# Down projection of a decoder layer: 20 of 22 row blocks in seven-product form, the third weight sum made in the block of the product ahead of it

## The chip, the cores and the metric

The kernel runs on one core of a Trainium2 chip. The metric is the device time of one execution in microseconds; the median of three runs is given. The profile is of one more execution.

## The reference

One decoder layer in float32: x is 512 rows of 1024. A token-mixing part (three attention branches, gated and projected) is followed by a gated MLP. The change lies in the last product of the MLP:

```python
x = x + rmsnorm(merged @ w_out[l], norm_mix_post[l])
h = rmsnorm(x, norm_ffn_pre[l])
u = causal_depthwise_conv(h @ w_ffn_up[l], ffn_conv_w[l], ffn_conv_b[l])
u_gate, u_val = jnp.split(u, 2, axis=-1)
y = (jax.nn.gelu(u_gate, approximate=True) * u_val) @ w_ffn_down[l]
x = x + rmsnorm(y, norm_ffn_post[l])
```

The hidden width is 2816, so `w_ffn_down` is 2816 x 1024: 22 row blocks of 128.

## The kernel before

All large products run on TensorE in split precision. A float32 operand is divided into a high part (ScalarE, line 85) and a rest (VectorE, line 86), and each product is three matmuls: high x high, high x rest, rest x high (`mm3`, `down3`). An instruction multiplies 128 x 128 by 128 x 512.

**Down projection.** Output is 512 rows (four blocks t of 128) by two halves h of 512 columns; each (t, h) has a PSUM bank. The first 16 of the 22 row blocks are taken in four groups d of four (NG = 4). Within a group the product is written as a 2 x 2 block product, and the seven-product form of Strassen and Winograd replaces eight block products by seven. A plain group of four row blocks is 4 x 4 x 2 x 3 = 96 matmuls; in the seven-product form it is 7 x 12 = 84. Product n of group d is called (n, d). The order is written out by hand in `seq`: products 1, 5, 6, 2, 7, 3, 4, each for all groups, then the six plain blocks (n = 0).

The sums of activations that the form needs are made on POOL in `sums` (lines 783 to 790), right after the last of a group's four blocks in the up projection: tile G holds the blocks (`gpair`), tile S three sums (`gsum`). The sums of weights are made by DMA: a quarter of a group (128 x 1024 in SBUF, 512 KB) is loaded on SP's queue, and `add_in` (line 859) lets a DMA on POOL's queue add another quarter from HBM into the same tile. Products 1, 5, 6, 4 of a group share one tile, `chain[d]`: it is loaded for 1, and after the split of 1, 5 and 6 the next quarter is added. Products 2, 7, 3 and the plain blocks take the four slots of `raw2` in turn; for product 7 a quarter is loaded into a slot and a second one added to it (lines 873 and 877).

`prepare(i)` issues loads up to three products ahead (`fetch_down`), then splits the weights (tiles whi and wlo, three buffers) and the activations (xh, xl). `upto(i + 2)` runs it two products ahead of TensorE. After the last group of product 1, 5, 6 and 7 ScalarE or VectorE reads the product's banks (lines 942 to 948) into `s_`, `z5` and `u2`, from which the output is put together.

The plain blocks come last. The last four (LATE = 4) are split into tiles of their own and are multiplied row block by row block, in the order t = 2, 3, 0, 1, so that norm, residual and store of one row block (lines 963 to 971) run beside the matmuls of the next.

The order of TensorE's instructions is that of the text. On the other engines the tile framework orders the instructions by a simulation of its own when the program is built, so they can leave the order of the text. The tiles named hT (two buffers) hold the activations of the up projection until its last matmul; after that `raw2` and `xlate` take their place.

Of the kernel before, what the change touches and what calls it, by code (L numbers as in the profile page):

```python
# [11 lines left out]
F32 = mybir.dt.float32  # L12
F32R = mybir.dt.float32r
# [6 lines left out]
P = 128  # L20
# [7 lines left out]
EPS = 1e-6  # L28
BIG = 1e30
VLEN = 640  # L30
LATE = 4
EARLY = 4
NG = 4
NS = 4 * NG
C_QMB, C_KMB, C_VMB, C_QSW, C_KSW, C_QME = 0, 512, 1024, 1536, 2048, 2304
C_GMB, C_GSW, C_GME = 2816, 3840, 4864
# [3 lines left out]
def tile_hybrid_layer(  # L40
# [734 lines left out]
    gpair = [T(fp, [P, 4, SEQ], F32, "G", NG) for _ in range(NG)]  # L775
    gsum = [T(fp, [P, 3, 2, 256], F32, "S", NG) for _ in range(NG)]
    grest = T(fp, [P, NF - NS, SEQ], F32, "gN", 1)

    def quarters(d):

        return [[gpair[d][:, r::2, c * 256 : (c + 1) * 256] for r in range(2)] for c in range(2)]

    def sums(d):

        (a11, a12), (a21, a22) = quarters(d)
        s1, s2, s4 = (gsum[d][:, i] for i in range(3))
# [26 lines left out]
    for f in range(NF):  # L813
        if f == 0:
            for k, banks in enumerate(zip(up_products(0), up_products(1))):
                if k + 4 < KD:
                    turn1(k + 4)
            issue(b_up[EARLY + 1])
        else:
            banks = [list(up_products(2 * f))[-1]]  # L820
        cg = conv(2 * f, banks[0])
        act.activation(cg[:], cg[:], AF.Gelu_apprx_tanh)  # L822
        if f:
            banks.append(list(up_products(2 * f + 1))[-1])
# [23 lines left out]
    u2 = [c_tile() for _ in range(2)]  # L848
    chain = {}
    loaded = {}  # L850
    turn = [0]
# [6 lines left out]
    def add_in(tile_, d, r, c):  # L858
        pool.dma_start(two(tile_), quarter(d, r, c), accum_op=ALU.add)

    seq = [(n, d) for n in (1, 5, 6, 2, 7, 3, 4) for d in range(NG)] + [(0, k) for k in range(NS, NF)]
    first_of = {2: (1, 0), 3: (1, 1), 7: (0, 1)}

    def fetch_down(i):
        n, d = seq[i]
        if n == 1:
            chain[d] = T(wp, [P, 1024], F32, "raw", 4)[:]
            sp.dma_start(two(chain[d]), quarter(d, 0, 0))
        elif n in first_of or n == 0:
            loaded[i] = raw2[:, turn[0] % 4, :]  # L870
            turn[0] += 1
            if n:
                sp.dma_start(two(loaded[i]), quarter(d, *first_of[n]))
            else:
                sp.dma_start(loaded[i], wd[d * P : (d + 1) * P, :])
            if n == 7:
                add_in(loaded[i], d, 1, 1)

    ready = {}
    fetched = [0]  # L880
# [1 line left out]
    def prepare(i):  # L882

        while fetched[0] <= min(i + 3, len(seq) - 1):
            fetch_down(fetched[0])
            fetched[0] += 1
        n, d = seq[i]
        w = loaded.pop(i) if i in loaded else chain[d]
        late = n == 0 and d >= NF - LATE
        if late:  # L890
            both = T(fp, [P, 2048], F32R, "G", NG)
            wh, wl = both[:, 0:1024], both[:, 1024:2048]
            q = d - (NF - LATE)
            xh, xl = xlate[:, q, 0:512], xlate[:, q, 512:1024]
        else:
            wh, wl = T(wp, [P, 1024], F32R, "whi", 3)[:], T(wp, [P, 1024], F32R, "wlo", 3)[:]
            xh, xl = T(fp, [P, 512], F32R, "xh", 3)[:], T(fp, [P, 512], F32R, "xl", 3)[:]
        split(wh, wl, w)
        if n == 0:
            split(xh, xl, grest[:, d - NS, :])  # L900
        else:
            (a11, a12), (a21, a22) = quarters(d)
            s1, s2, s4 = (gsum[d][:, q] for q in range(3))
            split(two(xh), two(xl), {1: a11, 2: a12, 3: s4, 4: a22, 5: s1, 6: s2, 7: a21}[n])
# [17 lines left out]
    def down(i, t, h, end=False):  # L922
        wh, wl, xh, xl = ready[i]
        c, a = slice(h * 512, (h + 1) * 512), slice(t * P, (t + 1) * P)
        down3(bank[t][h], xh[:, a], xl[:, a], wh[:, c], wl[:, c], seq[i][1] == NS and t > 1 and h == 1, end)

    into = {1: (0, 0), 2: (0, 0), 5: (0, 1), 3: (0, 1), 6: (2, 0), 7: (2, 0), 4: (2, 0)}
    for i, (n, d) in enumerate(seq):
        upto(i + 2)
        if n == 0:  # L930
            break
        wh, wl, xh, xl = ready.pop(i)
        t0, h = into[n]
        for j in range(2):
# [4 lines left out]
        if d == NG - 1:  # L939
            for p in range(2):  # L940
                if n == 1:
                    act.activation(s_[p], bank[p][0][:], AF.Copy)
                elif n == 5:
                    dve.tensor_tensor(z5[p], bank[p][1][:], s_[p], op=ALU.subtract)
                elif n == 6:
                    dve.tensor_tensor(u2[p][:], bank[2 + p][0][:], s_[p], op=ALU.add)
                elif n == 7:
                    dve.tensor_tensor(z5[p], z5[p], bank[2 + p][0][:], op=ALU.subtract)

    order = (2, 3, 0, 1)  # L950
    base = len(seq) - (NF - NS)
    for i in range(base, len(seq) - LATE):
        upto(i + 2)
        for t in order:
            for h in range(2):
                down(i, t, h)
    upto(len(seq))
    for t in order:
        for h in (1, 0):
            for i in range(len(seq) - LATE, len(seq)):  # L960
                down(i, t, h, i == len(seq) - 1)
            if t > 1:
                part = z5[t - 2] if h else s_[t - 2]
                dve.tensor_tensor(part, part, bank[t][h][:], op=ALU.add)
            elif h:
                dve.tensor_tensor(u2[t][:], bank[t][1][:], u2[t][:], op=ALU.subtract)
        r, ys = post_norm((s_[t - 2], z5[t - 2]) if t > 1 else (bank[t][0][:], u2[t][:]), gffn)
        for h in range(2):
            y = ys[h]
            dve.scalar_tensor_tensor(y[:], y[:], r[:], x1[t][h][:], op0=ALU.mult, op1=ALU.add)  # L970
            (sp if h else act).dma_start(out2[t * P : (t + 1) * P, h * 512 : (h + 1) * 512], y[:])


# [40 lines left out]
```

## Time and profile before

| | |
|---|---|
| time, median of 3 runs | 838.31 us (838.18 to 838.38) |
| time of the profiled execution | 838.42 us |
| its span, first to last instruction | 836.6 us |
| TensorE busy | 818.5 us, 98% of the span, 3967 matmuls |
| VectorE, ScalarE, POOL busy | 491.5, 395.3, 122.5 us |
| granted TensorE clock, mean | 0.994 |
| DMA | 94.52 MB, mean 113 GB/s |

The span is shorter than the time by what lies ahead of the first and behind the last instruction. Busy TensorE counts matmuls whose ends are modelled and which overlap, so the distance between the starts of two matmuls tells more than their durations. A granted clock of 1.0 is 2.4 GHz, one of 0.5 is 1.2 GHz.

### The profile page before, as it was taken

What the parts mean: (1) busy time and instruction counts of PE and PEld (TensorE: products, weight loads), DVE (VectorE), ACT (ScalarE), POOL (GpSimd) and SP (SyncE); (2) the same over time, 40 slices, a digit from 0 to 9 for tenths busy, and PEclk for the clock granted to TensorE, in tenths of its full rate; (3) what the DMA queues carried; (4) which work ended last, traced back from release to release, by engine and by line L of the source; (5) the groups of instructions that cost most, each with busy time, mean ns of one, the idle gap of its engine ahead of it and who ended that gap; (6) DMA issues with size and microseconds to landing.
All of it is one profiled execution on the core that took longest, in us unless ns stands there. A gap on an engine that the chain in (4) does not pass through costs nothing.

```text
span 836.6 us, 10565 instructions
## 1 busy us (share of the span) xinstructions
PE 818.5 (98%) x3967; PEld 688.4 (82%) x3967; DVE 491.5 (59%) x819; ACT 395.3 (47%) x687; POOL 122.5 (15%) x104
## 2 busy tenths in 40 slices
PE   6999999999999999999999999999999999998996
PEld 6888888888888888888888898888888888886885
DVE  5846566667658565545454755554445554784836
ACT  6735555556656555433343353343433333754621
POOL 5000000000001010122122211304141412421001
PEclk9999999999999999999999999999999999998999
DMA  9733222323333322233462223233333333999312
GB/s 299 226 92 86 66 83 89 89 81 101 92 86 101 89 88 89 89 101 117 146 206 60 77 72 104 87 91 100 101 101 101 93 89 95 223 229 229 100 51 100
DMA packets 123521, 94.52 MB, mean 113 GB/s; under 512 B 3559, under 2 KB 107183, under 8 KB 123471
## 3 DMA queue, kind: packets, MB, share of 16 engines
q1 hardware_dynamic: 118495, 84.40, 33.5%
q0 software_dynamic: 4352, 8.39, 5.8%
q10 hardware_dynamic: 624, 1.06, 0.3%
q8 instruction: 31, 0.51, 0.3%
q14 instruction: 19, 0.16, 0.1%
HBM read 91.70 MB, written 2.14 MB: 112 GB/s over the span
## 4 chain that ended last, share of the span: by engine, by line
PE 95%; DMA 2%; issue 1%; DVE 1%; ACT 0%; SPq 0%; DVEq 0%; POOLq 0%; POOL 0%; ACTq 0%
PE pj L129 22%; PE pj L130 22%; PE pj L131 22%; PE t L462 2%; PE s L487 2%; DMA hT<-in_w_ffn_down_dram 2%; PE s L919 1%; PE s L920 1%; PE s L918 1%; PE t L919 1%; PE t L918 1%; PE t L920 1%; PE o L471 1%; PE o L470 1%; PE o L919 1%
## 5 line engine op out<-in xcount | busy, mean ns | idle before, releaser
L129 PE MATMUL pj<-hT,whi 128*128 128x512 f32 (+1 forms) x704 | 273.8, 389 | 0.0
L130 PE MATMUL pj<-hT,whi 128*128 128x512 f32 (+1 forms) x704 | 271.0, 385 | 0.0
L131 PE MATMUL pj<-hT,wlo 128*128 128x512 f32 (+1 forms) x704 | 271.0, 385 | 0.0
L86 DVE TENSOR_TENSOR wlo<-raw,whi 128x1024 fp32r<-128x1024 f32 x123 | 158.3, 1287 | 176.8 <-ACT whi L85 176.6
L85 ACT ACTIVATE whi<-raw 128x1024 fp32r<-128x1024 f32 x127 | 134.4, 1059 | 177.2 <-PE pj L130 131.6
L131 PEld LDWEIGHTS pj<-hT,wlo 128*128 128x128 f32 x704 | 132.3, 188 | 26.8
L129 PEld LDWEIGHTS pj<-hT,whi 128*128 128x128 f32 x704 | 132.4, 188 | 24.3
L130 PEld LDWEIGHTS pj<-hT,whi 128*128 128x128 f32 x704 | 132.5, 188 | 24.1
L603 POOL TENSOR_TENSOR mx<-mx,gt 128x512 f32<-128x512 f32 x16 | 23.0, 1437 | 379.2 <-DVE gt L602 379.2
L129 PE MATMUL pj<-oT,whi 128*128 128x512 f32 (+1 forms) x128 | 48.1, 376 | 0.0
L130 PE MATMUL pj<-oT,whi 128*128 128x512 f32 (+1 forms) x128 | 47.1, 368 | 0.0
L131 PE MATMUL pj<-oT,wlo 128*128 128x512 f32 (+1 forms) x128 | 46.9, 367 | 0.0
L85 ACT ACTIVATE pt<-t 128x512 fp32r<-128x512 f32 (+2 forms) x48 | 24.3, 543 | 36.9 <-PE t L462 36.8
L827 POOL TENSOR_TENSOR G<-c,c 128x512 f32<-128x512 f32 x16 | 20.6, 1289 | 135.0 <-DVE c L810 117.2
L86 DVE TENSOR_TENSOR pt<-t,pt 128x512 fp32r<-128x512 f32 (+2 forms) x48 | 28.5, 621 | 19.9 <-ACT pt L85 19.5
L489 ACT ACTIVATE P<-P,tiny 128x256 f32<-128x256 f32 (+1 forms) x64 | 33.0, 517 | 14.0 <-DVE tiny L488 13.8
L822 ACT ACTIVATE c<-c 128x512 f32<-128x512 f32 x22 | 13.9, 632 | 42.9 <-DVE c L810 42.9
L810 DVE SCALAR_TENSOR_TENSOR c<-pj,convw,c 128x510 f32<-128x510 f32 x40 | 30.0, 750 | 1.4
L808 ACT ACTIVATE c<-pj,convw 128x512 f32<-128x512 f32 x40 | 30.4, 760 | 0.0
L809 DVE SCALAR_TENSOR_TENSOR c<-pj,convw,c 128x511 f32<-128x511 f32 x40 | 29.7, 743 | 0.0
L918 PE MATMUL s<-whi,xh 128*128 128x512 f32 x62 | 24.7, 399 | 3.3 <-ACT whi L85 3.3
L131 PEld LDWEIGHTS pj<-oT,wlo 128*128 128x128 f32 x128 | 24.6, 192 | 3.8
(346 smaller groups left out, 1283.2 us busy)
## 6 DMA issues: line engine op xcount, KB each, us to landing
raw<-in_w_in_dram SPq DMA_DIRECT2D x46, 512.0 KB, 3.9
raw<-in_w_ffn_up_dram SPq DMA_DIRECT2D x44, 512.0 KB, 3.8
hT<-in_w_ffn_down_dram SPq DMA_DIRECT2D x18, 512.0 KB, 5.2
raw<-in_w_ffn_down_dram POOLq DMA_DIRECT2D x12, 512.0 KB, 7.6
raw<-in_w_mem_kv_dram SPq DMA_DIRECT2D x8, 512.0 KB, 6.1
raw<-in_w_out_dram SPq DMA_DIRECT2D x8, 512.0 KB, 3.5
mx<-in_x_dram SPq DMA_DIRECT2D x12, 256.0 KB, 4.9
raw<-in_w_branch_mem_dram SPq DMA_DIRECT2D x4, 512.0 KB, 3.4
```

The lines of the kernel that those rows point to most:

```text
L85: act.activation(hi, src, AF.Copy)
L86: eng.tensor_tensor(lo, src, hi.bitcast(F32), op=ALU.subtract)
L129: pe.matmul(ps, wh, xh, start=start, stop=False)
L130: pe.matmul(ps, wh, xl, start=False, stop=False)
L131: pe.matmul(ps, wl, xh, start=False, stop=stop)
L489: act.activation(dst, dst, AF.Exp, bias=mn[:, i : i + 1], scale=-1.0, accum_out=sm[:, i : i + 1])
L603: pool.tensor_tensor(merged[c][:], merged[c][:], g[:], op=ALU.add)
L808: act.activation(c[:], ps[:], AF.Identity, scale=convw[:, 88 + ch : 89 + ch], bias=convw[:, 132 + ch : 133 + ch])
L809: dve.scalar_tensor_tensor(c[:, 1:512], ps[:, 0:511], convw[:, 44 + ch : 45 + ch], c[:, 1:512], op0=ALU.mult, op1=ALU.add)
L810: dve.scalar_tensor_tensor(c[:, 2:512], ps[:, 0:510], convw[:, ch : ch + 1], c[:, 2:512], op0=ALU.mult, op1=ALU.add)
L918: pe.matmul(ps[:], xh, wh, start=st, stop=False, skip_group_check=True)
L919: pe.matmul(ps[:], xh, wl, start=False, stop=False, skip_group_check=True)
```

## The change

NG goes from 4 to 5: 20 row blocks in seven-product form, two plain ones. The order of the products becomes 1, 5, 6, 3, 7, 4 for all five groups, then the two plain blocks, then product 2 for all groups, and after it the plain blocks' share of the banks (0, 0) and (1, 0).

- Product 3's quarter is loaded into `raw2[d]`, and after its split the quarter (0, 1) is added there for product 7. Then product 2's quarter is loaded into it. The quarter for product 4 is added to `chain[d]` in the text behind the split of product 7 instead of product 6.
- There are five `raw2` tiles and, for the fifth group, a `chain` tile and a tile of sums, all in the two hT buffers. The sums of the fifth group stand in the text behind the up projection.
- The plain blocks are loaded into `chain[0]` and `chain[1]` and split into buffers of S. Their matmuls for the rows 256 to 511 (both halves) and for the second half of the rows 0 to 255 stand ahead of product 2, and so do `finish` and `put` of the rows 256 to 511. The last matmuls are six for bank (0, 0) and six for (1, 0), each followed by its `finish` and `put`.
- G is laid out so that each quarter of a group is contiguous.

```diff
-LATE = 4
-NG = 4
+NG = 5
...
-        pool.tensor_tensor(gpair[f // 4][:, f % 4, :] if f < NS else grest[:, f - NS, :], cg[:], cv[:], op=ALU.mult)
-        if f < NS and f % 4 == 3:
+        if f < NS:
+            halves2 = lambda ap: ap.rearrange("p (c n) -> p c n", c=2)
+            pool.tensor_tensor(gpair[f // 4][:, f % 2 :: 2, f % 4 // 2, :], halves2(cg[:]), halves2(cv[:]), op=ALU.mult)
+        else:
+            pool.tensor_tensor(grest[:, f - NS, :], cg[:], cv[:], op=ALU.mult)
+        if f < NS - 4 and f % 4 == 3:
             sums(f // 4)
...
-    raw2 = T(mp, [P, 4, 1024], F32, "hT", 2)
-    xlate = T(mp, [P, LATE, 1024], F32R, "hT", 2)
+    big = [T(mp, [P, KD * SEQ], F32, "hT", 2) for _ in range(2)]
+    part = [b[:, q * 1024 : (q + 1) * 1024] for b in big for q in range(4)]
+    raw2, last_chain = part[0:5], part[5]
+    gsum.append(big[1][:, 2048 : 2048 + 1536].rearrange("p (a c) -> p a c", c=512))
+    sums(NG - 1)
...
-    seq = [(n, d) for n in (1, 5, 6, 2, 7, 3, 4) for d in range(NG)] + [(0, k) for k in range(NS, NF)]
-    first_of = {2: (1, 0), 3: (1, 1), 7: (0, 1)}
+    seq = [(n, d) for n in (1, 5, 6, 3, 7, 4) for d in range(NG)]
+    seq += [(0, k) for k in range(NS, NF)] + [(2, d) for d in range(NG)]
...
-            chain[d] = T(wp, [P, 1024], F32, "raw", 4)[:]
+            chain[d] = T(wp, [P, 1024], F32, "raw", 4)[:] if d < 4 else last_chain
             sp.dma_start(two(chain[d]), quarter(d, 0, 0))
...
+        elif n == 3:
+            sp.dma_start(two(raw2[d]), quarter(d, 1, 1))
+        elif n == 2:
+            sp.dma_start(two(raw2[d]), quarter(d, 1, 0))
+        elif n == 0:
+            sp.dma_start(chain[d - NS], wd[d * P : (d + 1) * P, :])
...
-        follow = {1: (0, 1), 5: (1, 1), 6: (1, 0)}.get(n)
-        if follow:
-            add_in(chain[d], d, *follow)
+        if n in (1, 5):
+            add_in(chain[d], d, *{1: (0, 1), 5: (1, 1)}[n])
+        elif n == 3:
+            add_in(raw2[d], d, 0, 1)
+        elif n == 7:
+            add_in(chain[d], d, 1, 0)
...
+    def finish(t, h, src):
+        junk = T(mp, [P, 512], F32, "o", 3)
+        act.activation(junk[:], src, AF.Square, scale=1.0 / math.sqrt(D), accum_out=sq[t][:, h : h + 1])
+        y = T(mp, [P, 512], F32, "gt" if h else "op", 2)
+        dve.tensor_tensor(y[:], src, gffn[h][:], op=ALU.mult)
+        scaled_y[t, h] = y
+    def put(t):
+        r = root(sq[t])
+        for h in range(2):
+            y = scaled_y[t, h]
+            dve.scalar_tensor_tensor(y[:], y[:], r[:], x1[t][h][:], op0=ALU.mult, op1=ALU.add)
+            (sp if h else act).dma_start(out2[t * P : (t + 1) * P, h * 512 : (h + 1) * 512], y[:])
...
         if n == 0:
-            break
+            if d == NF - 1:
+                for t in (2, 3):
+                    for h in range(2):
+                        rest(t, h)
+                        part_ = z5[t - 2] if h else s_[t - 2]
+                        dve.tensor_tensor(part_, part_, bank[t][h][:], op=ALU.add)
+                        finish(t, h, part_)
+                    put(t)
+                for t in (0, 1):
+                    rest(t, 1)
+                    dve.tensor_tensor(u2[t], bank[t][1][:], u2[t], op=ALU.subtract)
+                    finish(t, 1, u2[t])
+            continue
...
+    for t in (0, 1):
+        rest(t, 0)
+        finish(t, 0, bank[t][0][:])
+        put(t)
```

`rest(t, h)` issues the six matmuls of the two plain blocks into bank (t, h).

## Rows read from the trace of the kernel before

**Rows 1.** The page's part 2: the span in 40 equal slices of 20.9 us, busy share in tenths; TensorE, its granted clock, the DMA engines.
```profile
PE   6999999999999999999999999999999999998996
...
PEclk9999999999999999999999999999999999998999
DMA  9733222323333322233462223233333333999312
```

**Rows 2.** TensorE's instructions in order of time, six of the down projection: start us, duration us, what; in brackets the idle time before it and what ended it. 713.42 is the first matmul of the stretch, 829.54 the last.
```profile
713.42 0.39 PE L918 MATMUL s<-whi,xh 128*128 128x512 f32 x1
...
724.35 0.39 PE L918 MATMUL t<-whi,xh 128*128 128x512 f32 x1
...
735.00 0.39 PE L920 MATMUL t<-whi,xl 128*128 128x512 f32 x1
...
756.76 0.39 PE L920 MATMUL s<-whi,xl 128*128 128x512 f32 x1
...
760.44 0.50 PE L918 MATMUL s<-whi,xh 128*128 128x512 f32 x1 [3.30 <-ACT whi L85]
...
829.54 0.39 PE L920 MATMUL s<-G,hT 128*128 128x512 f32 x1
```

**Rows 3.** Table by stretch: the stretch, its length, busy us and count of each engine (PE, PEld, DVE, ACT, POOL), granted clock of TensorE, share of the DMA engines, GB/s. The first row is the start of the down projection, the others the stretch around its longest gap.
```profile
716.00:720.00 4.00, 4.00 (x20) 3.30 (x19) 4.00 (x6) 3.32 (x6) 2.80 (x2) 1.00 1.05 365
...
757.10:760.40 3.30, 0.05 (x1) 0.00 (x0) 0.00 (x0) 1.07 (x2) 1.20 (x1) 1.00 1.13 200
760.40:767.90 7.50, 6.70 (x16) 5.09 (x17) 5.57 (x6) 3.79 (x6) 0.00 (x0) 0.55 1.10 254
```

**Rows 4.** The chain of waits that ended last, in order of time, for the first product of form 7: start us, us, what.
```profile
741.18 1.05 ACT whi L85
...
743.51 8.19 DMA hT<-in_w_ffn_down_dram
...
752.24 6.99 DMA hT<-in_w_ffn_down_dram
759.33 1.07 ACT whi L85
```

**Rows 5.** DMA issues of two stretches, 705 to 712 us and 713 to 715.5 us: what, queue, count, size, median us from issue to landing.
```profile
raw<-in_w_ffn_down_dram POOLq DMA_DIRECT2D x2, 512.0 KB, 5.8
...
hT<-in_w_ffn_down_dram SPq DMA_DIRECT2D x4, 512.0 KB, 7.7
```

**Rows 6.** ScalarE's instructions in order of time, two splits that waited for a block added by DMA; two more like them lie between (731.31 and 733.83).
```profile
728.79 1.06 ACT L85 ACTIVATE whi<-raw 128x1024 fp32r<-128x1024 f32 x1 [1.12 <-DMA raw<-in_w_ffn_down_dram]
...
736.36 1.06 ACT L85 ACTIVATE whi<-raw 128x1024 fp32r<-128x1024 f32 x1 [0.53 <-DMA raw<-in_w_ffn_down_dram]
```

**Rows 7.** Groups of instructions by line from 690 us on: line, engine, operation, tiles, count | busy us, mean ns of one | idle time before and what ended it. Split of a weight block and of an activation block, on VectorE and on ScalarE.
```profile
L86 DVE TENSOR_TENSOR wlo<-raw,whi 128x1024 fp32r<-128x1024 f32 x18 | 22.0, 1222 | 17.8 <-ACT whi L85 17.8
L85 ACT ACTIVATE whi<-raw 128x1024 fp32r<-128x1024 f32 x18 | 19.0, 1055 | 14.4 <-PE pj L130 10.3 <-DMA raw<-in_w_ffn_down_dram 4.2
...
L86 DVE TENSOR_TENSOR xl<-S,xh 128x512 fp32r<-128x512 f32 x12 | 8.2, 686 | 1.2 <-ACT xh L85 1.2
...
L85 ACT ACTIVATE xh<-S 128x512 fp32r<-128x512 f32 x12 | 7.6, 632 | 6.6 <-PE o L919 3.7 <-PE t L919 1.4 <-PE s L919 1.3
```

**Rows 8.** POOL's instructions in order of time: the first and the last of the four sums of one group in the up projection (lines 787 to 790), and two of its instructions at the start of the down projection.
```profile
566.35 1.29 POOL L787 TENSOR_TENSOR S<-G 128x512 f32<-128x512 f32 x1
...
571.20 1.28 POOL L790 TENSOR_TENSOR S<-G,S 128x512 f32<-128x512 f32 x1
...
716.02 1.20 POOL L859 DMA_DIRECT2D raw<-in_w_ffn_down_dram  x1 [4.22 <-DVE wlo L86]
718.39 1.60 POOL L827 TENSOR_TENSOR gN<-c,c 128x512 f32<-128x512 f32 x1 [1.17 <-DVE c L810]
```

**Rows 9.** VectorE's instructions in order of time: a split in the up projection, a split at the start of the down projection, the first read of the banks of product 5, and the two of product 6.
```profile
567.61 1.23 DVE L86 TENSOR_TENSOR wlo<-raw,whi 128x1024 fp32r<-128x1024 f32 x1 [2.77 <-ACT whi L85]
...
718.75 1.78 DVE L86 TENSOR_TENSOR xl<-G,xh 128x512 fp32r<-128x512 f32 x1
...
736.06 0.69 DVE L944 TENSOR_TENSOR P<-t,P 128x512 f32<-128x512 f32 x1
...
746.12 0.68 DVE L946 TENSOR_TENSOR c<-s,P 128x512 f32<-128x512 f32 x1
746.72 0.68 DVE L946 TENSOR_TENSOR c<-o,P 128x512 f32<-128x512 f32 x1
```

**Rows 10.** The end of the kernel, ScalarE and then VectorE in order of time: what follows the last matmul.
```profile
830.03 0.60 ACT L703 ACTIVATE o<-s 128x512 f32<-128x512 f32 x1 [4.14 <-PE s L920]
...
830.75 0.69 DVE L707 TENSOR_TENSOR op<-s,gffn 128x512 f32<-128x512 f32 x1 [1.26 <-ACT o L703]
831.36 0.16 DVE L245 SCALAR_TENSOR_TENSOR tiny<-tiny 128x1 f32<-128x1 f32 x1
832.18 0.75 DVE L970 SCALAR_TENSOR_TENSOR op<-op,tiny,mx 128x512 f32<-128x512 f32 x1 [0.66 <-POOL tiny L246]
832.85 0.74 DVE L970 SCALAR_TENSOR_TENSOR gt<-gt,tiny,mx 128x512 f32<-128x512 f32 x1
```

More of the change, by code (lines that the diff above doesn't have):

```diff
@@ L774, in tile_hybrid_layer @@
     c_next = [c_tile()]
-    gpair = [T(fp, [P, 4, SEQ], F32, "G", NG) for _ in range(NG)]
-    gsum = [T(fp, [P, 3, 2, 256], F32, "S", NG) for _ in range(NG)]
+    gpair = [T(fp, [P, 4, 2, 256], F32, "G", NG) for _ in range(NG)]
+    gsum = [T(fp, [P, 3, 512], F32, "S", NG - 1)[:] for _ in range(NG - 1)]
     grest = T(fp, [P, NF - NS, SEQ], F32, "gN", 1)
     def quarters(d):
-        return [[gpair[d][:, r::2, c * 256 : (c + 1) * 256] for r in range(2)] for c in range(2)]
+        return [[gpair[d][:, 2 * c + r].rearrange("p j c -> p (j c)") for r in range(2)] for c in range(2)]
     def sums(d):
         (a11, a12), (a21, a22) = quarters(d)
-        s1, s2, s4 = (gsum[d][:, i] for i in range(3))
+        s1, s2, s4 = (gsum[d][:, i, :] for i in range(3))
         pool.tensor_tensor(s1, a21, a22, op=ALU.subtract)
@@ L847, in tile_hybrid_layer @@
     z5 = [t[:, 512:1024] for t in keep]
-    u2 = [c_tile() for _ in range(2)]
+    u2 = [c_tile()[:] for _ in range(2)]
     chain = {}
-    loaded = {}
-    turn = [0]
     def quarter(d, r, c):
@@ L866, in fetch_down @@
         if n == 1:
-            chain[d] = T(wp, [P, 1024], F32, "raw", 4)[:]
+            chain[d] = T(wp, [P, 1024], F32, "raw", 4)[:] if d < 4 else last_chain
             sp.dma_start(two(chain[d]), quarter(d, 0, 0))
[L869 to L877, printed above, removed]
+        elif n == 3:
[4 more added lines that the diff above has]
+            sp.dma_start(chain[d - NS], wd[d * P : (d + 1) * P, :])
     ready = {}
@@ L887, in prepare @@
         n, d = seq[i]
[L888 to L894, printed above, removed]
+        if n == 0:
+            q = d - NS
+            w = chain[q]
+            both = [T(fp, [P, 1536], F32R, "S", NG - 1) for _ in range(2)]
+            wh, wl = (b[:, 0:1024] for b in both)
+            xh, xl = (b[:, 1024:1536] for b in both)
+            x = grest[:, q, :]
         else:
+            w = raw2[d] if n in (2, 3, 7) else chain[d]
             wh, wl = T(wp, [P, 1024], F32R, "whi", 3)[:], T(wp, [P, 1024], F32R, "wlo", 3)[:]
             xh, xl = T(fp, [P, 512], F32R, "xh", 3)[:], T(fp, [P, 512], F32R, "xl", 3)[:]
+            (a11, a12), (a21, a22) = quarters(d)
+            s1, s2, s4 = (gsum[d][:, q, :] for q in range(3))
+            x = {1: a11, 2: a12, 3: s4, 4: a22, 5: s1, 6: s2, 7: a21}[n]
         split(wh, wl, w)
[L899 to L904, printed above, removed]
-        follow = {1: (0, 1), 5: (1, 1), 6: (1, 0)}.get(n)
-        if follow:
-            add_in(chain[d], d, *follow)
+        split(xh, xl, x)
+        if n in (1, 5):
[4 more added lines that the diff above has]
+            add_in(chain[d], d, 1, 0)
         ready[i] = (wh, wl, xh, xl)
@@ L920, in down3, with rest @@
         pe.matmul(ps[:], xl, wh, start=False, stop=end, skip_group_check=True)
-    def down(i, t, h, end=False):
-        wh, wl, xh, xl = ready[i]
+    def rest(t, h, end=True):
         c, a = slice(h * 512, (h + 1) * 512), slice(t * P, (t + 1) * P)
-        down3(bank[t][h], xh[:, a], xl[:, a], wh[:, c], wl[:, c], seq[i][1] == NS and t > 1 and h == 1, end)
+        for i in range(NG * 6, NG * 6 + NF - NS):
+            wh, wl, xh, xl = ready[i]
+            k = seq[i][1]
+            down3(bank[t][h], xh[:, a], xl[:, a], wh[:, c], wl[:, c], k == NS and t > 1 and h == 1, end and k == NF - 1)
+    sq = {t: tiny(2) for t in range(TT)}
+    scaled_y = {}
+    def finish(t, h, src):
[10 more added lines that the diff above has]
+            (sp if h else act).dma_start(out2[t * P : (t + 1) * P, h * 512 : (h + 1) * 512], y[:])
     into = {1: (0, 0), 2: (0, 0), 5: (0, 1), 3: (0, 1), 6: (2, 0), 7: (2, 0), 4: (2, 0)}
@@ L945, in tile_hybrid_layer @@
                 elif n == 6:
-                    dve.tensor_tensor(u2[p][:], bank[2 + p][0][:], s_[p], op=ALU.add)
+                    dve.tensor_tensor(u2[p], bank[2 + p][0][:], s_[p], op=ALU.add)
                 elif n == 7:
                     dve.tensor_tensor(z5[p], z5[p], bank[2 + p][0][:], op=ALU.subtract)
[L950 to L971, printed above, removed]
+    for t in (0, 1):
+        rest(t, 0)
+        finish(t, 0, bank[t][0][:])
+        put(t)
 _INS = ["x", "mem", "norm_mix_pre", "norm_mix_post", "norm_ffn_pre", "norm_ffn_post", "norm_mem",
```

## The prediction

> **What bounds the kernel now.** I read the slices of the page first: TensorE is at nine tenths in all but a few slices, and in slice 37 it falls, with its clock, while the DMA engines stand at nine tenths in the three slices up to there [rows 1]. So the kernel is bound by the number of matmuls, and by one break. That break lies in the down projection, the stretch that the change rewrites. In TensorE's own order of instructions that stretch runs from 713.42 to 829.54 us [rows 2], 480 matmuls (28 products of 12, six plain blocks of 24). An undisturbed pair of neighbours shows the pace: from 724.35 to 735.00 lie 47 steps, 0.2266 us each [rows 2]. 479 steps at that pace are 108.5 us; the stretch took 116.1, so 7.6 us are lost, and nearly all at one place: between 756.76 and 760.44 no matmul starts, the next one comes 1.26 us later, and after that the clock is at its lower level (1.2 GHz, a granted 0.55 on average from 760.4 to 767.9) [rows 2, 3].
>
> The chain of waits says why [rows 4]. That matmul is the first of product 7 of group 0. Its weight sum is made in two transfers: a block is loaded into raw2 (only after product 2 of the same group has been split and its slot is free, 743.51), which takes 8.19 us, and then a second block is added into it by an accumulating DMA on POOL's queue (752.24, 6.99 us). Only then ScalarE splits (759.33), and VectorE after it. From the split of product 2 that frees the slot to that of product 7 lie four products, 4 x 12 x 0.2266 = 10.9 us; the two transfers need over 15.
>
> **The change part by part.** *Matmuls.* One more group of four row blocks goes from 96 plain matmuls to 84: 468 instead of 480, 12 x 0.2266 = **-2.7 us**. Nothing hides this: TensorE is the chain.
>
> *The stall at product 7.* Product 3 now loads its block into raw2[d] (five slots, all free from the start of the stretch), and product 7 adds one more block into the same tile. The load is thus taken out of the wait, and five products, 13.6 us, lie between the split of (3,d) and that of (7,d). An add that meets an idle queue lands 5.8 us after its issue [rows 5], and the longest wait in the old chain, 6.99 us, also fits [rows 4]. So the stall goes, and the low clock after it: **-7.6 us**. What is late next is weighed below.
>
> *Adds and loads.* Adds rise from 16 to 20, loads fall from 22 to 17. When the queue is full, ScalarE's waits for added blocks end from 728.79 to 736.36 in three steps, 2.52 us per add [rows 6]; a product of TensorE takes 2.72. So adds keep up, if barely. For product 5 there is more room than before (five products instead of four between the split of (1,d) and that of (5,d)). POOL issues four more adds; its time between them is idle. I take 0.
>
> *Splits.* There are 37 instead of 34. Each costs ScalarE 1.06 + 0.63 and VectorE 1.22 + 0.69 us [rows 7], under the 2.72 us of a product: hidden by TensorE. If the cover went, three more would cost 3 x 1.9 = 5.7 us.
>
> *The sums of the fifth group* move to the end of the up projection, since their tile lies in the buffer that the last up product reads. Four POOL operations, 6.1 us from 566.35 to the end of the last at 572.48 [rows 8], then sit in front of the adds (1,2) and (1,3), which went out from 716.02 on. POOL does not follow the order of the text: it issued (1,2)'s add before the product of the last block, which stands earlier in the text [rows 8]. So the adds of (1,0) and (1,1) go out before the stretch, as now. Add (1,2) goes at about 721 instead of 716, lands near 727, and product (5,2), now at 713.4 + 7 x 2.72 = 732.4, needs it by 730: nothing lost, 3 us of margin.
>
> *The fifth block of product 1* has no slot in the raw ring. It is loaded when the up projection ends (713.4) and is needed by ScalarE at 723, for TensorE at 724.3. The first four loads of that moment landed after a median 7.7 us [rows 5]; first in its queue it is in time. Behind four others it is not (first rival). I take 0.5 us for this and the crowd around it; bounds 0 and 7.6 us, the old stall.
>
> *A new wait: product 7 is now followed at once by product 4, into the same PSUM banks,* and VectorE must have read product 7's result in between. Before, product 3 lay there. After product 6 VectorE's two reads began at 746.12 and 746.72 [rows 9]; the next product began at 713.42 + 144 x 0.2266 = 746.05. Had it needed those banks, it would have waited for the first read to end, 746.80: 0.75 us (its second bank is then free in time). Bounds: with VectorE free, the bank is complete 0.5 us before the product's end and a read of 0.68 follows: 0.3; with a split ahead of it as after product 5, where the reads began at 736.06 against a start at 735.23: 1.5. The row after product 6 is nearest: **+0.75 us**.
>
> *The end.* Before, the last block of 128 rows had 24 matmuls (5.4 us) to itself, and after its last matmul came: square 830.03, gain 830.75, root 831.36, power, two final operations 832.18 and 832.85 to 833.59 [rows 10]. These stay; the second square, which goes, is no loss or gain, since the root follows the gain operation. But now two blocks finish 6 matmuls, 1.36 us, apart, and VectorE has 2.2 us of work for each. If the second block's gain goes first, the end is 0.7 us later; if it waits for the first block's two final operations, 1.5. I take **+1.0**. The rows 256 to 511 finish earlier and beside product 2; their VectorE work, 11 us within 22 us that also hold 9.5 us of splits, fits, with 0 to 1.5 us at risk, for which I take 0.
>
> Sum: -2.7 - 7.6 + 0.5 + 0.75 + 1.0 = -8.05. The profiled execution took 838.42 us (836.6 of span and 1.8 around it), 0.1 above the median of the runs: 838.42 - 8.05 = 830.4, and 830.3 on the median's scale.
>
> One thing speaks against the moved sums: POOL's product at 718.39 took 1.60 us, and the VectorE split that began beside it, at 718.75, took 1.78 [rows 8, 9] instead of 0.69 [rows 7]. But the split at 567.61, which ran beside the same four sums in the up projection, kept its 1.23 us [rows 8, 9]. So I count the sums as free for VectorE, and the pair at 718 as a rival (2). The Trainium skill (GPSIMD Engine Reference, Specifications) says that POOL shares its SBUF interfaces with VectorE and that VectorE instructions with two SBUF inputs meet contention there. The trace agrees at 718.75 and not at 567.61; by the rule rival 2 would be the forecast, 832.0 instead of 830.3.
>
> **The rivals.** (1) *The block for (1,4) queues behind those of product 3.* Both wait for buffers freed within one matmul of each other. If four loads of product 3 are issued first, it lands two and a half loads after their median (714.2 + 7.7 [rows 5]); loads moved at some 365 GB/s from 716 to 720 [rows 3], 1.44 us for each 0.524 MB, so near 725.5. TensorE then waits some 3.8 us, VectorE's half included, and the clock falls as it did before, for 2.9 us (16 matmuls in 7.5 us [rows 3], less 3.6 at the full pace and 1.0 of waiting): 6.2 us net of the 0.5 above, 836.5; with two or three ahead 831 to 833. For it: four loads went out at this moment before [rows 5]. Against: in the text it comes first. 0.17.
> (2) *POOL's sums slow VectorE.* Four collisions at 1.1 us, 4.4, less the 2.7 us of late splits that no longer stand there: product (1,3) or (1,4) starts 1.7 us late: 832.0. For it and against it the two rows above. 0.08.
> (3) *The stall moves to product 5*: POOL takes the sums first and adds (1,0) after them, at 720; it lands at 727, product (5,0) would start then and needs 2.4 us more for its split, plus the low clock, 2.9: 833 to 836. Against: POOL's order above. 0.09.
> (4) *Slower: adds become the pace.* All twenty products that need an add then run at the add's interval. At 2.52 us nothing happens; each 0.1 us over 2.72 costs 2 us, and from 3.13 on (8 us) the gain is gone; at 3.3 it is 842. For it: an add that shares the engines with loads lands later (6.99 us [rows 4] against 5.8 [rows 5]). Against: loads run beside adds for some 10 us at the start only. 0.04.
> (5) *The sum rewritten does nothing*, because the second transfer is still late: then only -2.7 and +1.75 remain, 837.5. Against: 13.6 us for one transfer. 0.03.
>
> **How the numbers follow.** My forecast has 0.59, with its own range 828.0 (no new cost at all: -10.3) to 832.5. The likeliest gives 830.3. Rivals 2 and the mild forms of 1 and 3 reach 835; I leave out their hard forms, 4 and 5, together somewhat under 2 in 10. Range 828.0 to 835.0. Within 0.2% of 838.3 (836.6 to 840.0, about what a measurement of this kernel can tell from no change) fall hard 1 and 5: 0.06. Slower is rival 4: 0.04. Faster: 0.90.
>
> **What would show it.** After: 468 matmuls in the stretch, at 0.227 us, from its start to its last in some 107 us; no wait over 1 us and no low clock near product 7; a wait of TensorE for VectorE's read of product 7 at its end, 0.3 to 1.5 us; last matmul near 820; the last store 7 to 8 us after it. I am wrong if TensorE waits at (1,4) for a load, at (5,d) or (6,d) for an add, or if the clock falls anywhere in the stretch.

## The result: 832.22 us, and the profile after

The changed kernel takes 832.22 us (median of four runs, 831.93 to 833.2) against 838.24 (837.9 to 838.38) for the kernel before: ratio 0.9931, 95% interval 0.9914 to 0.9948. The forecast was 830.3 with a range of 828 to 835. It fell by 6.0 us where 8.05 had been worked out.

The page's part 2 of the changed kernel, in the form of [rows 1]:

```profile
PE   6999999999999999999999999999999999999996
PEclk9999999999999999999999999999999999999999
DMA  9632222323332233324354214323333333899602
```

The break in slice 37, and the drop of the clock with it, are gone. TensorE's own instructions, in the form of [rows 2], with the two places where it still waits in the down projection:

```profile
714.62 0.39 PE L921 MATMUL s<-whi,xh 128*128 128x512 f32 x1
...
722.78 0.39 PE L921 MATMUL s<-whi,xh 128*128 128x512 f32 x1
724.34 0.50 PE L922 MATMUL s<-wlo,xh 128*128 128x512 f32 x1 [1.17 <-DVE wlo L85]
...
783.87 0.39 PE L923 MATMUL o<-whi,xl 128*128 128x512 f32 x1
784.93 0.47 PE L921 MATMUL s<-whi,xh 128*128 128x512 f32 x1 [0.68 <-DVE P L984]
...
822.87 0.39 PE L923 MATMUL s<-S,S 128*128 128x512 f32 x1
```

From the first to the last matmul lie 108.25 us, 7.88 less than before. 467 steps of 0.2266 us are 105.8, so 2.4 are still lost: between 722.78 and 724.34, in the middle of product (1,3), 1.44 us over the pace with the step after it, and between 783.87 and 784.93, ahead of (4,0), 0.9. The same two waits stand in the list of what TensorE waited for in the whole run; the others of that length are at the kernel's start:

```profile
PE t L271 <- DMA gt<-in_norm_ffn_pre_dram: 5.8, 1, 5.8
PE s L922 <- DVE wlo L85: 1.2, 1, 1.2
PE s L266 <- DMA mx<-in_mem_dram: 0.8, 1, 0.8
PE s L921 <- DVE P L984: 0.7, 1, 0.7
```

From the last matmul's start to the end of the span it is 8.13 us, 7.10 before. The profiled execution took 833.2 us, the slowest of the four. Its down projection starts 1.2 us later than in [rows 2]. That delay is of this execution: a second profile of the changed kernel (told with the last experiment below) starts it at 713.05 and runs it in 108.24. The balance of the two profiled executions is then +1.2 ahead of the stretch, -7.88 in it, +1.02 behind it and +0.4 outside the span, -5.2 together. So what the change saves is saved inside the stretch, and what fell short of the sum lies for the most part at the first of the two waits (1.44 us lost, where 0.5 had been allowed for the start) and in the 0.4 outside the span.

### The profile page after: what moved, and what is told of

Its sections match the earlier page's. It is cut to its first block, busy times and chain, and to the rows that moved or that the text cites. A ratio compares the mean times of both kernels' runs of the same rounds, so it can differ in the third digit from the quotient of the medians.

```text
span 831.0 us, 10570 instructions
## 1 busy us (share of the span) xinstructions
PE 814.0 (98%) x3955; PEld 685.1 (82%) x3955; DVE 501.1 (60%) x825; ACT 399.4 (48%) x693; POOL 133.2 (16%) x112
## 2 busy tenths in 40 slices
DMA packets 123761, 93.99 MB, mean 113 GB/s; under 512 B 3543, under 2 KB 107167, under 8 KB 123711
## 4 chain that ended last, share of the span: by engine, by line
PE 96%; DVE 2%; DMA 1%; ACT 0%; issue 0%; SPq 0%; DVEq 0%; ACTq 0%
PE pj L128 22%; PE pj L129 22%; PE pj L130 22%; PE t L461 2%; PE s L486 2%; PE s L922 2%; PE s L921 2%; PE s L923 2%; PE t L922 1%; PE t L921 1%; PE t L923 1%; PE o L470 1%; PE o L469 1%; DVE wlo L85 1%; PE o L922 1%; PE o L921 1%
## 5 line engine op out<-in xcount | busy, mean ns | idle before, releaser
L85 DVE TENSOR_TENSOR wlo<-raw,whi 128x1024 fp32r<-128x1024 f32 x123 | 161.5, 1314 | 175.4 <-ACT whi L84 175.3
L828 POOL TENSOR_TENSOR G<-c,c 128x512 f32<-128x512 f32 x20 | 25.7, 1286 | 167.2 <-DVE c L809 149.4
L922 PE MATMUL s<-wlo,xh 128*128 128x512 f32 x70 | 27.4, 391 | 1.2 <-DVE wlo L85 1.2
L129 PEld LDWEIGHTS pj<-oT,whi 128*128 128x128 f32 x128 | 25.0, 196 | 4.1 <-DVE oT L88 0.8
```

Source lines behind the costliest of these rows:

```text
L85: eng.tensor_tensor(lo, src, hi.bitcast(F32), op=ALU.subtract)
L129: pe.matmul(ps, wh, xl, start=False, stop=False)
L828: pool.tensor_tensor(gpair[f // 4][:, f % 2 :: 2, f % 4 // 2, :], halves2(cg[:]), halves2(cv[:]), op=ALU.mult)
```

## The experiments

Each ratio below is to the kernel before, timed on the same chip as the experiment. The first four experiments and the last ran on one chip, where the changed kernel takes 831.72 us; the three others ran on another, and the changed kernel was not timed beside them.

Theory: the gain is all of the weight sum of product 7, and the fifth group's 2.7 us are given back at three places: at (1,3), where POOL's late sums hold up VectorE's split; ahead of (4,0), where the banks of product 7 are read; and at the end. Rivals: the wait at (1,3) is for a block or an added block that comes late; the gain comes from fewer matmuls and the new order, with the sum only a part of it; and the low clock alone, not the transfer, was the loss.

What VectorE and POOL did around (1,3) is what the first experiment starts from. VectorE in the changed kernel:

```profile
718.45 1.59 DVE L85 TENSOR_TENSOR xl<-G,xh 128x512 fp32r<-128x512 f32 x1
719.97 4.32 DVE L85 TENSOR_TENSOR wlo<-raw,whi 128x1024 fp32r<-128x1024 f32 x1
724.21 0.68 DVE L85 TENSOR_TENSOR xl<-G,xh 128x512 fp32r<-128x512 f32 x1
```

POOL in the same stretch: the four moved sums, and then the up projection's last product:

```profile
714.72 1.28 POOL L786 TENSOR_TENSOR hT<-G 128x512 f32<-128x512 f32 x1 [1.73 <-PE pj L129]
716.08 2.16 POOL L787 TENSOR_TENSOR hT<-hT,G 128x512 f32<-128x512 f32 x1
718.20 1.30 POOL L788 TENSOR_TENSOR G<-G 128x512 f32<-128x512 f32 x1
...
720.21 1.75 POOL L789 TENSOR_TENSOR hT<-G,hT 128x512 f32<-128x512 f32 x1
721.46 1.73 POOL L830 TENSOR_TENSOR gN<-c,c 128x512 f32<-128x512 f32 x1
```

A split of 1.22 us [rows 7] took 4.32, and ended 1.1 us after the last of these POOL operations (721.46 + 1.73 = 723.19). ScalarE had finished `whi` at 718.90, before the split began, so the block was there.

**The fifth group's sums early.** Their tile is moved to three buffers that are free during the up projection, so POOL makes them there, like those of the other groups.

```diff
-    gsum.append(big[1][:, 2048 : 2048 + 1536].rearrange("p (a c) -> p a c", c=512))
-    sums(NG - 1)
+    gsum.append([T(mp, [P, 512], F32, "o", 3)[:] for _ in range(3)])
...
-        if f < NS - 4 and f % 4 == 3:
+        if f < NS and f % 4 == 3:
```

> The changed kernel, with one edit: the three sums of the fifth group stand in the three buffers named o, which are free during the up projection, so POOL makes them there, as for the other four groups, and not at the start of the down projection. Theory: TensorE's wait of 1.3 us at product (1,3) in the changed kernel comes from POOL: the VectorE split of (1,3) began at 719.97, while POOL had the last sum and the last up product in front of it, and took 4.3 us instead of 1.2. Then here that split takes under 2 us, the wait at (1,3) is under 0.3 us, and the time falls by about 1.4 us, to 830.8. Rival: the split is slow because six blocks are loaded into the same memory from 714 to 727. These loads stay, so the split still takes over 3 us and the time stays at 832.2.

Measured: 830.82 us (830.48 to 831.44, six runs), ratio 0.9925 (0.9910 to 0.9941). The stretch runs from 712.90 to 819.67, 106.77 us, 1.48 less than with the change as built; the time is 0.9 less than the changed kernel's on this chip. Of TensorE's waits the one for `wlo` is gone and the other stays:

```profile
PE s L920 <- DVE P L983: 0.7, 1, 0.7
```

The split that stands where the 4.32 us were, on VectorE, and the one POOL operation that is left beside it:

```profile
717.20 2.25 DVE L85 TENSOR_TENSOR wlo<-raw,whi 128x1024 fp32r<-128x1024 f32 x1
```

```profile
716.79 1.59 POOL L831 TENSOR_TENSOR gN<-c,c 128x512 f32<-128x512 f32 x1
```

The same split took 1.22 us alone, 2.25 beside one POOL operation and 4.32 beside two, and beside either it ended 1.1 us, about its own length, after the last of them. So the wait at (1,3) is POOL's work, and no transfer. From the last matmul's start to the end of the span it took 8.73 us instead of 8.13; what is known of that stands under the third experiment.

**A product between 7 and 4.** (2,0) is put between (7,4) and (4,0).

```diff
-    seq = [(n, d) for n in (1, 5, 6, 3, 7, 4) for d in range(NG)]
-    seq += [(0, k) for k in range(NS, NF)] + [(2, d) for d in range(NG)]
+    seq = [(n, d) for n in (1, 5, 6, 3, 7) for d in range(NG)] + [(2, 0)] + [(4, d) for d in range(NG)]
+    seq += [(0, k) for k in range(NS, NF)] + [(2, d) for d in range(1, NG)]
```

> The changed kernel, with one edit: product (2,0) is taken out of the last five and stands between (7,4) and (4,0). It writes other banks than 7 and 4. Theory: the gap of 1.06 us ahead of (4,0) is TensorE waiting until VectorE has read product 7's result; with 2.7 us of other matmuls between them it is gone, and the time falls by 0.9 us, to 831.3. Rival: the gap is the split of (4,0) being late (the trace also names ScalarE's split of the activations); then a gap of about 1 us stays ahead of (2,0) or (4,0) and the time stays at 832.2.

Measured: 831.81 us (831.23 to 832.15, six runs), ratio 0.9935 (0.9920 to 0.9949). The stretch takes 107.32 us, 0.93 less, and TensorE's only wait in it is the one at (1,3):

```profile
PE s L922 <- DVE wlo L85: 1.2, 1, 1.2
```

The wait ahead of (4,0) is thus the read of product 7's banks and costs 0.9 us of the stretch. The time did not fall with it: 831.81 us, where the changed kernel takes 831.72 on this chip. The end of the span is 0.6 longer here (8.71 us), as in the first experiment.

**The end row by row.** The last product and the rest of each row block are multiplied for row block 0 first and then for 1, with norm and stores of 0 before the matmuls of 1.

```diff
+        last = i == len(seq) - 1
-        for j in range(2):
-            for p in range(2):
+        for j, p in ((0, 0), (1, 0), (0, 1), (1, 1)) if last else ((0, 0), (0, 1), (1, 0), (1, 1)):
...
+            if last and j == 1:
+                rest(p, 0)
+                finish(p, 0, bank[p][0][:])
+                put(p)
```

> The changed kernel, with one edit: the last product (2,4) is issued row block by row block, and each row block's six matmuls of the plain blocks follow its half, so that the two last row blocks finish 12 matmuls (2.7 us) apart instead of 6 (1.4 us). Theory: the end is 1.0 us longer than before because VectorE has 2.2 us of work for each of the two and they collide; with 2.7 us between them the end is as long as before, and the time falls by 0.6 to 1.0 us, to 831.4. Rival: the end is longer because of four stores close together, or of the row block's own chain; then the stretch from the last matmul to the end stays at 8.1 us and the time at 832.2.

Measured: 831.01 us (830.87 to 831.28, six runs), ratio 0.9926 (0.9912 to 0.9940). The stretch is unchanged at 108.25 us, and from the last matmul's start to the end of the span it takes 7.53 instead of 8.13. VectorE's last operations in the changed kernel, in the form of [rows 10]:

```profile
824.07 0.69 DVE L941 TENSOR_TENSOR op<-s,gffn 128x512 f32<-128x512 f32 x1 [0.60 <-ACT o L939]
824.68 0.15 DVE L244 SCALAR_TENSOR_TENSOR tiny<-tiny 128x1 f32<-128x1 f32 x1
824.75 0.74 DVE L948 SCALAR_TENSOR_TENSOR op<-op,tiny,mx 128x512 f32<-128x512 f32 x1
825.41 0.74 DVE L948 SCALAR_TENSOR_TENSOR gt<-gt,tiny,mx 128x512 f32<-128x512 f32 x1
826.07 0.74 DVE L948 SCALAR_TENSOR_TENSOR op<-op,tiny,mx 128x512 f32<-128x512 f32 x1
826.74 0.74 DVE L948 SCALAR_TENSOR_TENSOR gt<-gt,tiny,mx 128x512 f32<-128x512 f32 x1
```

And in this experiment, whose last matmul started at 821.53:

```profile
822.11 0.74 DVE L948 SCALAR_TENSOR_TENSOR gt<-gt,tiny,mx 128x512 f32<-128x512 f32 x1
822.77 0.68 DVE L941 TENSOR_TENSOR op<-s,gffn 128x512 f32<-128x512 f32 x1
823.37 0.15 DVE L244 SCALAR_TENSOR_TENSOR tiny<-tiny 128x1 f32<-128x1 f32 x1
824.18 0.75 DVE L948 SCALAR_TENSOR_TENSOR op<-op,tiny,mx 128x512 f32<-128x512 f32 x1 [0.66 <-POOL tiny L245]
824.85 0.74 DVE L948 SCALAR_TENSOR_TENSOR gt<-gt,tiny,mx 128x512 f32<-128x512 f32 x1
```

In the changed kernel the first row block's two final operations (824.75, 825.41) stand in front of the second's, and the last operation ends 4.61 us after the last matmul's start (827.48 - 822.87). Here the first block is done before the second's gain begins, and it is 4.06 (825.59 - 821.53), as in the kernel before (833.59 - 829.54 = 4.05). So the row blocks finishing close together cost 0.55 us on VectorE. What remains of the end, from VectorE's last operation to the end of the span, holds the last stores: 3.06 us before, 3.51 in the changed kernel, 4.11 in the first and the second experiment, 3.47 here. It goes with the kernel and not with the execution: a second profile gives 3.52 for the changed kernel, and two profiles of the third sum alone (next) give 3.29 each. And the transfers themselves are over well before the span is. The table by stretch, from 829.4 us to the end in the changed kernel, and from 835.4 in the kernel before:

```profile
829.40:831.00 1.60, 0.00 (x0) 0.00 (x0) 0.00 (x0) 0.00 (x0) 0.00 (x0) 0.50 0.00 0
```

```profile
835.40:836.60 1.20, 0.00 (x0) 0.00 (x0) 0.00 (x0) 0.00 (x0) 0.00 (x0) 0.50 0.00 0
```

No engine works and the DMA engines move nothing. Of the +1.02 us at the end, then, 0.55 are the change's order, and 0.45 come behind VectorE's last operation, most of them in this empty time; no run says why. In the second experiment, 0.6 us more behind the last operation took back most of the 0.9 that the stretch had gained.

**The third sum alone.** The kernel before, with four groups and all 480 matmuls, only that product 3 comes ahead of 7, and product 7's quarter is added to the block loaded for product 3.

```diff
-    seq = [(n, d) for n in (1, 5, 6, 2, 7, 3, 4) for d in range(NG)] + [(0, k) for k in range(NS, NF)]
+    seq = [(n, d) for n in (1, 5, 6, 3, 7, 2, 4) for d in range(NG)] + [(0, k) for k in range(NS, NF)]
...
+        elif n == 3:
+            sp.dma_start(two(raw2[:, d, :]), quarter(d, 1, 1))
+        elif n == 2:
+            sp.dma_start(two(raw2[:, d, :]), quarter(d, 1, 0))
...
+        if n == 3:
+            add_in(raw2[:, d, :], d, 0, 1)
```

> The kernel before (16 row blocks in seven-product form, six plain, product 4 last of the seven), with the weight sums of the change alone: order 1, 5, 6, 3, 7, 2, 4; product 3 loads its block, product 7 adds one to it, product 2 is loaded there afterwards. Theory: the change's gain is the stall at product 7 that goes (7.6 us) and 12 matmuls (2.7 us), which are independent; this kernel has the first alone, 838.2 - 7.6 = 830.6, and no gap over 1 us in the down projection. That is less than the changed kernel's 832.2, since the sums on POOL, the wait between 7 and 4 and the longer end do not come with it. Rival: the stall went because there are fewer loads and five products between, not four; with four groups the add comes late too, a gap of 2 us or more stays at product 7 with the low clock behind it, and the time is 834 to 838.

Measured: 831.16 us (830.92 to 831.5, four runs), ratio 0.9928 (0.9910 to 0.9945). First and last matmul of its stretch:

```profile
713.42 0.39 PE L918 MATMUL s<-whi,xh 128*128 128x512 f32 x1
...
822.05 0.39 PE L920 MATMUL s<-G,hT 128*128 128x512 f32 x1
```

That is 108.63 us where 479 steps need 108.5: no wait, no low clock. This one edit, the sum with the order that it needs, gives at least as much as the whole change. The change as built needs 108.25 us for 12 matmuls less.

**A fresh block for product 7.** The changed kernel, with the old way of making that sum: load, then add.

```diff
+        elif n == 7:
+            sp.dma_start(two(raw2[d]), quarter(d, 0, 1))
+            add_in(raw2[d], d, 1, 1)
...
-        elif n == 3:
-            add_in(raw2[d], d, 0, 1)
```

> The changed kernel with the weight sum of product 7 made as before the change: after the split of (3,d) a block is loaded into raw2[d] and a second one added to it (two transfers), instead of one block added to the block that product 3 has just used (one transfer). All else is the changed kernel, five products between the two included. Theory: before the change the two transfers took over 15 us and had 10.9; here they have 13.6, less 2.3 for the split, so the add is still late: a gap of 2 to 5 us at (7,0), with the low clock behind it from about 3 us on, and the time is 834 to 839. Rival: the distance of five products and the free slots did it, not the sum in place; then there is no gap at product 7 and the time is 832.2 as in the changed kernel.

Measured: 838.31 us (838.02 to 838.93, ten runs), ratio 1.0013 (1.0002 to 1.0024). The stretch takes 114.69 us, 6.4 more. The order of the products is the changed one, so the gain is the sum's. The form of the loss was another than expected: not one long wait and a slow clock, but a wait inside four of the five products of form 7, 1.4 us ahead of product 4, and a full clock. Its waits in the down projection (the first line also counts the wait at (1,3), which this kernel shares with the changed one):

```profile
PE s L923 <- DVE wlo L85: 4.2, 5, 1.2
PE s L922 <- DVE P L985: 1.4, 1, 1.4
...
PE s L922 <- ACT whi L84: 0.2, 1, 0.2
```

One of the four, at (7,1); from start to start each is 1.26 or 1.27 us, where a step at full pace is 0.23:

```profile
773.20 0.50 PE L922 MATMUL s<-whi,xh 128*128 128x512 f32 x1
774.46 0.50 PE L923 MATMUL s<-wlo,xh 128*128 128x512 f32 x1 [0.76 <-DVE wlo L85]
```

The table by stretch, 764 to 790 us (columns as in [rows 3]), and below it the same stretch of the changed kernel:

```profile
764.00:790.00 26.00, 21.40 (x83) 14.94 (x83) 13.75 (x16) 11.89 (x15) 3.29 (x3) 1.00 0.98 239
```

```profile
764.00:790.00 26.00, 25.32 (x112) 20.68 (x111) 20.44 (x23) 16.64 (x21) 1.20 (x1) 1.00 0.75 203
```

29 matmuls fewer in 26 us, the granted clock at 1.00 (2.4 GHz) throughout, the DMA engines at 0.98. With loads and adds of product 7 both on the way, the sums come further apart than the products that need them. This kernel also moves one block per group more than the changed one (96.62 MB against 93.99), and the waits fall while its DMA engines are full. Whether the loss is the time of two transfers in a row or that of the added bytes is not parted by any run. A late sum costs about the same here, in several places at a full clock, as before the change, at one place with a low clock behind it (6.4 and 7.6 us).

**Product 3's blocks first.** The five loads for product 3 are issued ahead of that of (1,4), as the first rival of the prediction has it.

```diff
+    for d in range(NG):
+        sp.dma_start(two(raw2[d]), quarter(d, 1, 1))
     ready = {}
...
-        elif n == 3:
-            sp.dma_start(two(raw2[d]), quarter(d, 1, 1))
```

> The changed kernel, with the five loads for product 3 ahead of the load for (1,4) on SP's queue; in the changed kernel it is first. It prices the first rival of the prediction. Theory: loads of one queue land in order, some 1.5 to 2 us apart at that moment, so the block of (1,4) lands near 727 to 729 us where the split needs it at 723 to 724: a gap of 3 to 5 us at (1,4) instead of the 1.4 us at (1,3), the clock falls to its lower level for some us, and the time is 836 to 840. Rival: the queue's loads share the engines evenly, or the start has slack; then the gap stays under 2 us and the time at 832 to 833.

Measured: 838.28 us (837.44 to 843.29, ten runs), ratio 1.0019 (1.0005 to 1.0033); the stretch takes 114.28 us, 6.0 more. TensorE's waits in it, and the table by stretch around (1,4):

```profile
PE s L921 <- ACT whi L84: 3.1, 1, 3.1
PE s L922 <- DVE wlo L85: 1.9, 2, 1.2
...
PE s L921 <- DVE P L984: 0.7, 1, 0.7
```

```profile
725.30:728.70 3.40, 0.36 (x2) 0.00 (x0) 0.00 (x0) 1.04 (x2) 0.00 (x0) 1.00 1.05 190
728.70:733.80 5.10, 4.27 (x11) 3.13 (x12) 4.10 (x4) 2.62 (x5) 3.09 (x3) 0.67 0.38 52
733.80:740.00 6.20, 6.20 (x29) 5.12 (x28) 3.83 (x4) 4.33 (x7) 1.76 (x2) 1.00 1.12 204
```

TensorE stands idle for 3.1 us, then works with the clock at its lower level (1.2 GHz) for part of 728.7 to 733.8, a granted 0.67 on average, and is back at full speed after. The first rival's mechanism was right, and its price (6.2 us for four loads ahead) is close to the 6.0 measured with five ahead; only its condition did not hold: in the changed kernel the load for (1,4) was issued first, at 714.59.

**The three repairs together**: early sums, (2,0) between, and the end row by row.

> The changed kernel with the three edits of the earlier experiments together: the fifth group's sums made in the up projection, (2,0) between 7 and 4, and the last product issued row block by row block. Theory: the three costs are separate places, so the gains add up: no gap over 0.4 us in the down projection, 106 us from its first to its last matmul, 7.4 to 7.6 us from there to the end, and a time of 832.2 - 1.4 - 0.9 - 0.7 = 829.2. Rival: one takes from another (the sums of the fifth group in the buffers named o, or the earlier product 2, delay something at the end); then at least one of the gaps is back and the time is 830 or more.

Measured: 829.15 us (828.74 to 829.5, five runs), ratio 0.9907 (0.9894 to 0.9920), faster than the kernel before on the same chip, and lower than every time of the changed kernel (831.46 to 833.2), which was not timed beside it. Its first and last matmul:

```profile
712.84 0.39 PE L920 MATMUL s<-whi,xh 128*128 128x512 f32 x1
...
818.69 0.39 PE L922 MATMUL s<-S,S 128*128 128x512 f32 x1
```

105.85 us for 467 steps that need 105.8, and no wait of TensorE is left in the down projection. This is the 2.4 us found above, taken back. VectorE's last operation ends 4.06 us after the last matmul's start, so the end's 0.55 are back too; but the span ends 7.99 us after that start, not 7.4 to 7.6 as expected, since 3.93 follow VectorE's last operation. That the time met the 829.2 is therefore in part luck.

**The changed kernel and the third sum alone, side by side.** Both were timed once more on one chip, without edits.

> The changed kernel once more, on one chip with the kernel of the third sum alone, since the kernel before was timed from 835 to 840 us in the calls so far and the two have only been set side by side through it. Theory: in the changed kernel the fifth group's 2.7 us are given back at product (1,3) (1.4 us), ahead of product 4 (0.9) and at the end (0.6 to 1.0), so the changed kernel is 0.3 to 1.2 us slower than the third sum alone. Rival: the fifth group is worth its 12 matmuls, and the changed kernel is 1 us or more faster than the third sum alone on the same chip.

> The third sum alone (16 row blocks in seven-product form), the same kernel as in the earlier experiment, on the same chip as the changed kernel. Theory: 0.3 to 1.2 us faster than the changed kernel, near 831.2. Rival: 1 us or more slower than the changed kernel.

Measured: 831.72 us (831.46 to 831.92, four runs; 0.9921, 0.9907 to 0.9936) for the changed kernel, 831.38 (830.52 to 831.53, four runs; 0.9918, 0.9902 to 0.9935) for the third sum alone. The difference of 0.3 us lies at the lower edge of what was expected and inside both intervals: the two can't be told apart. Their spans agree as well, 829.2 to 829.7 against 828.8 to 829.8 us; the 0.4 by which they differ outside the span is told in the next section. That the change as a whole is a microsecond better than its one part is out. The second profile of the changed kernel shows the split at (1,3) again:

```profile
718.40 4.32 DVE L85 TENSOR_TENSOR wlo<-raw,whi 128x1024 fp32r<-128x1024 f32 x1
```

## Why the prediction was right, and where it was off

**Matmuls, -2.7.** Right as a count (468) and in the pace of the version with all three repairs, 105.85 us; but as built the 2.7 us are given back in whole by the terms below (the third sum alone has a stretch 0.4 us longer and an end 0.8 shorter).

**The stall at product 7, -7.6.** Right in size, and right that the sum in place takes the stall away. The third sum alone shortens the stretch from 116.13 to 108.63 us, 7.5; undoing it in the changed kernel costs 6.4. That five slots and five products in between would leave no wait at 7 is seen in TensorE's list of waits. The mechanism as the prediction has it, the time of two transfers in a row, rests on the chain in [rows 4]; the runs show that the sum in place takes the loss away, and leave open how much of it is the time in a row and how much the bytes of the second block.

**The start, +0.5.** Mis-sized: 1.44 us were lost there. The crowd of loads, for which the term stood, cost nothing; the loss is the second rival, POOL's moved sums beside VectorE's splits, which I had given 0.08 and 1.7 us. Two of the splits shown above, of 1.59 and 4.32 us, lost 4.0 together, where that rival had 4.4. The step that failed is the one that counted the sums as free for VectorE, on the strength of the split at 567.61 that kept its 1.23 us [rows 9]. That reading looked at one side of the pair only. The row of POOL's second sum, next to it in the trace of the kernel before:

```profile
567.72 2.26 POOL L788 TENSOR_TENSOR S<-S,G 128x512 f32<-128x512 f32 x1
```

2.26 us where its neighbours have 1.28 and 1.29 [rows 8]: here POOL waited for VectorE, and nothing waited for POOL. At the start of the down projection VectorE waited for POOL, and TensorE for VectorE. So the two rows that the prediction set against each other were the same contention, with the loss on either side. The Trainium skill (GPSIMD Engine Reference, Specifications) says that VectorE instructions with two SBUF inputs meet contention with POOL; by it rival 2 would have been the forecast, and 4.32 us against 1.22 agree with it. How much is lost, and by which of the two, came only from the rows.

**Four more adds and the splits, 0.** Right: TensorE's list has no wait in the down projection but the two.

**The wait between 7 and 4, +0.75.** Right: 0.9 us by the starts, and the first read, from 784.10 to 784.78, began at the very time at which the next product was due, as the row of product 6 in [rows 9] had it.

**The end, +1.0.** The number was right (1.02), and nearly half of it by luck: 0.55 us are the operations of two row blocks on VectorE, a little under the lower of the two bounds given (0.7), and 0.45 come behind VectorE's last operation, for which the sum had no term.

**Time outside the span.** It was taken as unchanged, a term put at nothing, and it is not: 2.2 us in all eight runs of the changed kernel (2.17 to 2.26), 1.7 to 1.85 in every run of the kernel before and of the third sum alone. So some 0.4 us belong to the change. No run here says why.

## What to carry to other kernels

A weight sum made by two transfers in a row needs the time of both between two uses; a block already loaded for an earlier product takes the first of them off the path and moves fewer bytes, and this alone gave the whole gain. Work that is moved to another engine's idle time is free only if it doesn't run beside two-input operations on which the critical engine hangs: a pair in which the critical engine kept its time proves nothing before the other engine's row beside it has been read. And before a change is credited with its parts, run the parts: here 12 matmuls less bought nothing until three losses of 0.5 to 1.5 us were taken out.

## What the runs showed of the hardware

- An operation of VectorE on two SBUF tiles and one of POOL on two SBUF tiles hardly ran at the same time: a split of 1.22 us took 2.25 beside one POOL operation of 1.59, and 4.32 beside two; in the up projection it was POOL's sum of 1.28 us that took 2.26. Which of the two waits is not settled. In five pairs it was mainly the one listed later that lost: VectorE's splits at 718.75 [rows 9], 717.20 and 718.45, behind POOL's operations at 718.39 [rows 8], 716.79 and 718.20, lost 1.1, 1.0 and 0.9 us; POOL's sums at 567.72 and 716.08, behind VectorE's splits at 567.61 and 715.69, lost 1.0 and 0.9. But the split of 4.32 us is listed 0.2 us ahead of the sum (719.97 and 720.21) and lost all the same, straight behind a VectorE operation that had itself been delayed.
- Four waits, each with 1.26 or 1.27 us between the starts of two matmuls, within 17 us left the granted clock at 1.00; an idle time of 3.1 us was followed by the lower level, as the one of 3.3 in [rows 2] and [rows 3] was.
- From VectorE's last operation to the end of the span it took 3.06 to 4.11 us in different kernels, and nearly the same in two executions of one (3.51 and 3.52, 3.29 and 3.29); at least the last 1.2 us of it before the change, and 1.6 after, are without any transfer.
- The kernel before spread from 835.25 to 839.29 us in eleven runs on one chip, and the kernel with product 3's blocks first from 837.44 to 843.29, both with a stretch at the lower clock; those without one kept within 1.3 us. That the clock's stretch is the reason was not tried.
